# Three paddings in the on-chip memory of a hybrid pooling and attention layer

## The chip, the cores and the metric

The kernel runs on one core of one Trainium2 chip. A core has TensorE (matmuls: a stationary operand, the weights, is loaded first, and a moving operand then streams past it), VectorE, ScalarE, GpSimd and a sync engine that issues most of the transfers. Operands of the engines lie in the on-chip memory, which has 128 partitions; a place in it is a number of bytes from the start of each partition. Matmul results go to eight banks of PSUM.

The metric is the device time of one execution in microseconds (us), lower is better. The kernel before takes 1139.48 us, the median of 3 runs (1139.41 to 1140.89).

## What is computed

One decoder layer in float32, on a sequence of 1,024 rows of 1,024 channels:

```python
h = rms_norm(x, ln_pre_mix[l])
proj = h @ w_in[l]
...
q, k = rope(q, pos), rope(k, pos)
pool_out = multi_scale_pool(u_pool, w_pool[l], pool_scale[l])
attn_out = dilated_attention(q, k, v).reshape(B, S, ATTN_WIDTH)
mix = jnp.concatenate([pool_out, attn_out], axis=-1) @ w_out[l]
x = x + rms_norm(mix, ln_post_mix[l])
h = rms_norm(x, ln_pre_ffn[l])
f = (jax.nn.silu(h @ w_gate[l]) * (h @ w_up[l])) @ w_down[l]
x = x + rms_norm(f, ln_post_ffn[l])
```

The pooling mixer takes 256 channels, the attention 12 heads of 64 channels, each under three windows and strides. The feed-forward part is 2,816 wide (22 tiles of 128).

## The kernel before

Channels lie on the partitions and positions along the free dimension. Each float32 operand is split into a high part, rounded to the type float32r, and a low part, the rest; a product is three float32r matmuls (high by high, high by low, low by high: `PASSES`, L331). A big matmul has 128 x 128 weights and a moving operand of 128 x 512, so 2,048 bytes in each partition.

The stages follow each other: the input projection with the statistics of the first normalisation, the twelve attention units (a pair of heads and half of the positions each) with projections of later pairs as filling work between them, the output projection, and the feed-forward part. The two big products of the feed-forward part are done in Strassen's manner with seven block products instead of eight: `seven` (L1471) has, for each of 11 pairs of tiles, seven products of 2 x 4 x 3 matmuls. Three of these have a block of the normalised input itself as the moving operand (tiles `b00`, `b10`, `b11`, made by `block`, L1336; the profile calls them `b`), four a sum of blocks (tiles `tT1` to `tT4`; the profile calls them `tT`). For the first six pairs (`EARLY`) two of the products are made ahead by `firsts` (L1367). `down` (L1799) has seven products of 11 x 4 x 3 matmuls with operands from `operands` (L1643), the last of them in halves of 256 columns. `out_proj` (L1154) has 8 x 8 x 3 matmuls for each half of the positions; for one tile of them, d = 3 of the second half, the weights lie in the block `b4` of the `ffnl` pool (L1160). `rows_first` (L933) has the rows of `x` as weights and the weight matrix as the moving operand; two of its eight k-tiles lie in `w3` (L928). `turn` (L848) turns the score tiles `pp` with `idt` or `pmt` as the moving operand.

Every matmul goes through the helper `mm` (L275), which keeps TensorE's instructions in the order in which the program writes them. Splits into high and low parts are spread over ScalarE, VectorE and GpSimd by hand, and the order around them comes from the planner's due times in `PRM`.

The on-chip memory is a stack from each end. Pools on the left are placed upward in the order in which they are opened, pools with `side="right"` downward from the top, and a pool is as big as what its tiles need. Each tile is rounded up to 32 bytes. In the compiled program the left side begins with 2,048 bytes of transfer scratch and four constants of the framework; behind them come `const` (half, eps, ones, idt, g2s, g3s, g4s: from 2,176), `wpool` (two `wraw` of 4,096 bytes, from 2,880), `small` (from 11,072) and then, from 13,216, first `con1` (g1s, qdA, qdB, ls0, ls1, pmt, rb, psc) and `att`, and in the feed-forward part `ffnl` (r3, the blocks b0 to b5, three `rw`, two `q`). In `con1`, `pmt` lies at 14,336, `rb` at 14,848 and `psc` at 18,944; `att` begins at 18,976. `idt` lies at 2,272. The `ffnl` blocks begin at 17,312 and are 8,192 bytes each.

On the right the top is at 229,344. From there down come `xg` (eight tiles of 8,192 bytes: first `x0` to `x7`, later `z`, `tT`, `op` and others in the same places), `hlp` (two `whl`), and then `qkp` (k, qh, ql, masks and others) or, in the feed-forward part, `mid` (four `fw`, `sq`, `p`, `rb` strips).

The lines that the change touches are the opening of the pools, the tile of ones for the sums of squares, and the load of the pooling scale:

```python
xgp = ctx.enter_context(tc.tile_pool(name="xg", bufs=1, side="right"))
...
ones = const.tile([P, 1], F32, name="ones")
...
psc = cload(pscale, [P, 2], "psc", con1)
```

Of the kernel before, what the change touches and what calls it, by code (L numbers as in the profile page):

```python
# [8 lines left out]
F32 = mybir.dt.float32  # L9
# [6 lines left out]
P = 128  # L16
# [254 lines left out]
def hybrid_block(ctx: ExitStack, tc: tile.TileContext, xT, w_in, w_v, w_vp, w_pool, w_out, w_gate, w_up, w_down,  # L271
                 g1, g2, g3, g4, pscale, cost, sint, maskA, maskB, quadA, quadB, lsel, ident, perm, band, out):
    nc = tc.nc
# [6 lines left out]

    const = ctx.enter_context(tc.tile_pool(name="const", bufs=1))
    wpool = ctx.enter_context(tc.tile_pool(name="wpool", bufs=1))
    xgp = ctx.enter_context(tc.tile_pool(name="xg", bufs=1, side="right"))
    hlp = ctx.enter_context(tc.tile_pool(name="hlp", bufs=1, side="right"))
    small = ctx.enter_context(tc.tile_pool(name="small", bufs=3))
# [15 lines left out]
    def cload(src, shape, name, pool=None, eng=nc.sync):  # L301
        t = (pool or const).tile(shape, F32, name=name)
        eng.dma_start(t, src)
        return t
# [47 lines left out]
    right, left = ExitStack(), ExitStack()  # L352
    con1 = left.enter_context(tc.tile_pool(name="con1", bufs=1))
# [8 lines left out]
    for h in range(2):  # L362
        for a in range(2):
            nc.gpsimd.memset(qlow[h][64 - 64 * a:128 - 64 * a, a].bitcast(F32), 0.0)
    ones = const.tile([P, 1], F32, name="ones")
    nc.vector.memset(ones, 1.0)
    warm = qkp.tile([P, 512], F32R, name="warm", tag="rsw", bufs=1)
    nc.vector.memset(warm.bitcast(F32), 0.0)
# [645 lines left out]
        did(("pool", h))  # L1014

    g2s, g3s, g4s = (cload(g, [P, NK], "g%ds" % (n + 2)) for n, g in enumerate((g2, g3, g4)))
    psc = cload(pscale, [P, 2], "psc", con1)

    def emit(*lists):

# [904 lines left out]
```

## Time and profile before

| what | value |
|---|---|
| median of 3 runs | 1139.48 us |
| the profiled execution's own time | 1139.3 us |
| its span, first to last instruction | 1137.5 us |
| mean granted TensorE clock | 0.997 |
| matmuls in the trace | 5922 |
| data moved by transfers | 201.59 MB, 177 GB/s over the span |

In the views, PE is TensorE's matmuls, PEld its weight loads, DVE VectorE, ACT ScalarE, POOL GpSimd. Matmuls overlap each other: the duration of one (about 390 ns for 512 columns) is longer than the distance from its start to the start of the next, and it is this distance, the pace, that fills the time. The pace is read from a run of equal matmuls: the start of the next group less the start of this one, divided by the number; or the length of a piece in the chain in order of time, divided by its number.

A row of matmuls names `out<-moving,stationary`. All tiles of one name share a row, and so do all tiles whose names differ only in their number.

### The profile page before, as it was taken

To read this page: it belongs to the slowest core of one execution; us is meant where nothing else is said; L and a number is where in the kernel's file an instruction comes from. 1 tells how busy PE (TensorE), PEld (TensorE's weight loads), DVE (VectorE), ACT (ScalarE), POOL (GpSimd) and SP (SyncE) were. 2 spreads that over 40 slices of the span, in tenths; PEclk is the share of its full clock that TensorE was granted. 3 is DMA by queue.
4 is the path that set the end of the run, shared out by engine and by line. 5 is a ranking of instruction groups with operands and counts; after the bars stand their busy time and mean duration, and the time that the engine had idled before them with its cause. 6 is when DMAs were issued, how large, how long until landed. Compare 5 with 4: busy or idle time off the path is not lost.

```text
span 1137.5 us, 16902 instructions
## 1 busy us (share of the span) xinstructions
PE 1120.4 (98%) x5922; PEld 958.1 (84%) x5922; DVE 807.6 (71%) x1516; ACT 559.1 (49%) x1068; POOL 550.6 (48%) x481
## 2 busy tenths in 40 slices
PE   9999999999999999999999999999999999999997
PEld 7888999999898888888888878888888888888896
DVE  7967888888998675989777777665676473343684
ACT  7466667666678573965422222322323434344441
POOL 0122646253465222010267667775577897666521
PEclk9999999999999999999999999999999999999999
DMA  8215242414147555773566666433544796566442
GB/s 280 93 70 186 83 141 75 149 57 167 56 131 246 181 200 193 291 254 123 188 231 231 232 231 231 167 141 142 190 167 167 272 351 222 192 203 192 141 149 74
DMA packets 91156, 201.59 MB, mean 177 GB/s; under 512 B 9280, under 2 KB 25152, under 8 KB 89664
## 3 DMA queue, kind: packets, MB, share of 16 engines
q1 hardware_dynamic: 90096, 199.74, 50.2%
q8 instruction: 46, 0.75, 0.3%
q10 hardware_dynamic: 976, 0.79, 0.2%
q14 instruction: 38, 0.31, 0.1%
HBM read 143.61 MB, written 56.89 MB: 176 GB/s over the span
## 4 chain that ended last, share of the span: by engine, by line
PE 87%; DVE 6%; POOL 3%; DMA 2%; issue 1%; ACT 1%; SPq 0%; ACTq 0%; DVEq 0%; POOLq 0%
PE ps_pj L276 28%; PE ps_s L276 25%; PE ps_o L276 22%; PE ps_t L276 10%; PE ps_t L279 3%; DMA rw<-in_w_up_dram 1%; POOL fw L1365 1%; POOL pp L814 1%; DVE pp L748 1%; DVE ptr L860 1%; DVE rsw L510 0%; POOL whl L1464 0%; DMA wraw<-in_w_in_dram 0%; ACT pp L751 0%; DVE ql L542 0%
## 5 line engine op out<-in xcount | busy, mean ns | idle before, releaser
L276 PE MATMUL ps_o<-tT,fw 128*128 128x512 f32 x648 | 150.9, 390 | 0.9 <-DVE sq L1548 0.9
L276 PEld LDWEIGHTS ps_o<-tT,fw 128*128 128x128 f32 x648 | 121.5, 188 | 26.9 <-issue 1.3
L276 PE MATMUL ps_pj<-x,whl 128*128 128x512 f32 x480 | 138.1, 407 | 0.3 <-DVE whl L322 0.3
L814 POOL TENSOR_SCALAR pp<-pp,wv 128x256 f32<-128x256 f32 (+1 forms) x135 | 67.8, 523 | 111.5 <-DVE wv L794 111.5
L1365 POOL TENSOR_TENSOR fw<-rw,fw 128x512 fp32r<-128x512 f32 x72 | 100.3, 1416 | 30.2 <-ACT fw L1363 30.1
L751 ACT ACTIVATE pp<-pp,sx 128x128 f32<-128x128 f32 (+1 forms) x192 | 89.3, 468 | 31.5 <-DVE sx L748 30.9
L276 PEld LDWEIGHTS ps_pj<-x,whl 128*128 128x128 f32 x480 | 85.0, 189 | 11.2 <-DVE whl L322 0.7
L348 POOL TENSOR_TENSOR nrr<-nrr,half 128x4 f32<-128x4 f32 (+1 forms) x7 | 7.9, 1124 | 145.5 <-ACT eps L347 103.8
L1660 POOL TENSOR_TENSOR op<-rw,op 128x512 fp32r<-128x512 f32 x38 | 62.3, 1638 | 32.5 <-ACT op L1659 32.5
L322 POOL TENSOR_TENSOR whl<-wraw,whl 128x512 fp32r<-128x512 f32 x42 | 54.7, 1327 | 45.3 <-ACT whl L318 45.3
L276 PE MATMUL ps_s<-b,fw 128*128 128x512 f32 x312 | 74.6, 394 | 0.0
L276 PEld LDWEIGHTS ps_s<-b,fw 128*128 128x128 f32 x312 | 58.5, 187 | 14.2
L1365 POOL TENSOR_TENSOR whl<-rw,whl 128x512 fp32r<-128x512 f32 x30 | 47.1, 1589 | 44.2 <-ACT whl L1363 30.1
L276 PE MATMUL ps_pj<-whl,x 128*128 128x256 f32 (+1 forms) x432 | 68.4, 299 | 0.0
L1363 ACT ACTIVATE fw<-rw 128x1024 fp32r<-128x1024 f32 x45 | 47.5, 1061 | 41.8 <-PE ps_o L276 17.8
L1659 ACT ACTIVATE op<-rw 128x1024 fp32r<-128x1024 f32 x38 | 40.0, 1058 | 56.4 <-PE ps_t L276 28.2
L860 DVE TENSOR_TENSOR ptr<-ps_t,ptr 128x512 fp32r<-128x512 f32 (+1 forms) x84 | 55.3, 665 | 12.1 <-ACT ptr L859 11.3
L859 ACT ACTIVATE ptr<-ps_t 128x512 fp32r<-128x512 f32 (+1 forms) x84 | 47.4, 578 | 27.9 <-PE ps_t L279 24.0
L276 PEld LDWEIGHTS ps_pj<-whl,x 128*128 128x128 f32 x432 | 58.2, 191 | 1.7
L1661 DVE TENSOR_TENSOR op<-rw,op 128x512 fp32r<-128x512 f32 x33 | 28.8, 872 | 40.1 <-ACT op L1659 29.9
L276 PE MATMUL ps_o<-ptr,v 128*128 128x128 f32 (+1 forms) x472 | 56.4, 257 | 0.2 <-DVE ptr L860 0.2
L276 PE MATMUL ps_s<-k,qh 128*128 128x128 f32 (+1 forms) x192 | 54.4, 295 | 1.9 <-DVE sx L748 1.5
(328 smaller groups left out, 2858.7 us busy)
## 6 DMA issues: line engine op xcount, KB each, us to landing
rw<-bd SPq DMA_DIRECT2D x77, 256.0 KB, 4.0
rw<-in_w_gate_dram SPq DMA_DIRECT2D x28, 512.0 KB, 4.3
rw<-in_w_up_dram SPq DMA_DIRECT2D x28, 512.0 KB, 5.9
v<-vd SPq DMA_DIRECT2D x22, 512.0 KB, 4.6
rw<-wsd SPq DMA_DIRECT2D x44, 256.0 KB, 3.8
bd<-p SPq DMA_DIRECT2D x39, 256.0 KB, 2.1
rw<-in_w_down_dram SPq DMA_DIRECT2D x33, 256.0 KB, 3.8
wraw<-in_w_out_dram SPq DMA_DIRECT2D x15, 512.0 KB, 4.8
```

Of the source, the lines that this page charges most:

```text
L276: return tc.keep_in_program_order(nc.tensor.matmul(*a, **k))
L279: return tc.keep_in_program_order(nc.tensor.transpose(dst, src, by))
L322: pin(eng.tensor_tensor(dst[:, 1, at:at + w], src[:, at:at + w], dst[:, 0, at:at + w].bitcast(F32), ALU.subtract))
L751: nc.scalar.activation(pt[:, j, lo:], pt[:, j, lo:], AF.Exp, bias=sx[:, 0, side, j, hd, 0:1], scale=-1.0, accum_out=sx[:, 0, side, j, hd, ...
L814: nc.gpsimd.tensor_scalar(pv, pv, un.wv[:, side, j, hd:hd + 1], 1.0, op0=ALU.mult, op1=ALU.mult)
L859: nc.scalar.activation(ptr[:, 0, :w], t[:, :w], AF.Copy)
L860: nc.vector.tensor_tensor(ptr[:, 1, :w], t[:, :w], ptr[:, 0, :w].bitcast(F32), ALU.subtract)
L1363: nc.scalar.activation(dst[:, :, 0], src, AF.Copy)
L1365: low[0] = eng.tensor_tensor(dst[:, i, 1], src[:, i], dst[:, i, 0].bitcast(F32), ALU.subtract)
L1659: nc.scalar.activation(w[:, :, 0], raw, AF.Copy)
L1660: nc.gpsimd.tensor_tensor(w[:, 0, 1], raw[:, 0], w[:, 0, 0].bitcast(F32), ALU.subtract)
L1661: (nc.gpsimd if p == "P1" else nc.vector).tensor_tensor(w[:, 1, 1], raw[:, 1], w[:, 1, 0].bitcast(F32), ALU.subtract)
```

## The change

Three tiles of padding are added. A pool `edge` with one tile of 504 floats (2,016 bytes), that nothing reads or writes, is opened on the right ahead of `xg`. The tile of ones becomes 281 floats wide, and its first column is used. The tile of the pooling scale becomes 98 floats wide, and its first two columns are used; its load is written out instead of through `cload` (L301), on the same queue and at the same place.

```diff
     const = ctx.enter_context(tc.tile_pool(name="const", bufs=1))
     wpool = ctx.enter_context(tc.tile_pool(name="wpool", bufs=1))
+    edge = ctx.enter_context(tc.tile_pool(name="edge", bufs=1, side="right"))
+    edge.tile([P, 504], F32, name="edge")
     xgp = ctx.enter_context(tc.tile_pool(name="xg", bufs=1, side="right"))
...
-    ones = const.tile([P, 1], F32, name="ones")
+    ones = const.tile([P, 281], F32, name="ones")[:, :1]
     nc.vector.memset(ones, 1.0)
...
     g2s, g3s, g4s = (cload(g, [P, NK], "g%ds" % (n + 2)) for n, g in enumerate((g2, g3, g4)))
-    psc = cload(pscale, [P, 2], "psc", con1)
+    psc = con1.tile([P, 98], F32, name="psc")[:, :2]
+    nc.sync.dma_start(psc, pscale)
```

## The prediction

> **What bounds the kernel now.** I read the page first, then the busy time by stretches, then the chain of waits in order of time, then TensorE's timeline and the matmuls grouped by form.
>
> ```profile
> span 1137.5 us, 16902 instructions
> PE 1120.4 (98%) x5922; PEld 958.1 (84%) x5922; DVE 807.6 (71%) x1516; ACT 559.1 (49%) x1068; POOL 550.6 (48%) x481
> PE 87%; DVE 6%; POOL 3%; DMA 2%; issue 1%; ACT 1%; SPq 0%; ACTq 0%; DVEq 0%; POOLq 0%
> ```
>
> TensorE is busy for 1120.4 of 1137.5 us and makes 87% of the chain that ended last. Whatever changes the pace of one matmul to the next changes the end; whatever changes another engine's pace must first use up that engine's idle time.
>
> ```profile
> 200.00:340.00 140.00, 138.12 (x910) 126.27 (x909) 121.51 (x346) 94.98 (x250) 61.59 (x81) 1.00 0.34 113
> 480.00:620.00 140.00, 140.00 (x627) 114.37 (x627) 114.37 (x160) 62.54 (x96) 45.02 (x34) 1.00 0.58 203
> 700.00:800.00 100.00, 100.00 (x437) 81.61 (x436) 67.39 (x74) 29.24 (x35) 68.31 (x50) 1.00 0.45 172
> 800.00:900.00 100.00, 100.00 (x437) 81.60 (x437) 60.50 (x63) 28.12 (x35) 71.69 (x52) 1.00 0.53 192
> ```
>
> The columns are PE, weight loads, VectorE, ScalarE, GpSimd, then the granted clock, here 1.00. Even between 200 and 340 us TensorE idles for only 1.88 of 140 us. From 480 us on, it has no gap in these stretches, and each matmul there costs its full pace. That pace is not one number. In the timeline (start, length, group) and in the chain in order of time (start, length, number) stand runs of 24 or 48 matmuls of one shape:
>
> ```profile
> 454.76 5.66 PE L276 MATMUL ps_s<-fw,b 128*128 128x512 f32 x24
> 465.69 5.60 PE L276 MATMUL ps_s<-fw,whl 128*128 128x512 f32 x24
> 586.24 5.60 PE L276 MATMUL ps_s<-tT,whl 128*128 128x512 f32 x24
> 591.68 11.04 PE L276 MATMUL ps_o<-tT,fw 128*128 128x512 f32 x48
> 602.56 5.76 PE L276 MATMUL ps_s<-b,fw 128*128 128x512 f32 x24
> 608.16 5.62 PE L276 MATMUL ps_o<-tT,fw 128*128 128x512 f32 x24
> ```
>
> ```profile
> 454.92 5.49 PE ps_s L276 x24
> 465.85 5.44 PE ps_s L276 x24
> 540.94 11.20 PE ps_s L276 x48
> 586.40 5.44 PE ps_s L276 x24
> 591.84 10.88 PE ps_o L276 x48
> 602.72 5.60 PE ps_s L276 x24
> ```
>
> The names after the arrow are the moving tile, then the stationary one. With `tT` or `fw` moving, 24 matmuls take 5.44 us, 226.7 ns each. With `b` moving they take 5.60 us (48 take 11.20), 233.3 ns each. With `fw` moving and `b` stationary they take 5.49 us, 228.8 ns. The 48 `tT` matmuls at 591.84 and the 24 `b` matmuls that follow differ in nothing that the profile shows but the moving tile: both have `fw` as weights. The PSUM tag does not decide, since `ps_s` appears at both paces.
>
> What differs is where the tiles lie. The compiled program of the kernel before has every big right-hand tile (`x`, `tT`, `op`, `fw`, `whl`, `k`, `qh`) 2,016 bytes past a multiple of 2,048, the `ffnl` tiles (`b`, `rw`, `r3`) 928 past one, the `att` tiles (`pp`, `ptr`, `v`, `w3`) 544 past one. Weights start 512 bytes apart within their tile, so the distance from weights to moving tile, modulo 512, is 0 for right on right (226.7 ns), 448 for `b` moving over right (233.3 ns), and 64 for right over `b` (228.8 ns). A third pair has distance 64, `w3` moving over `x`:
>
> ```profile
> 53.43 2.91 PE L276 MATMUL ps_pj<-w,x 128*128 128x512 f32 x12
> 56.18 1.08 PE L276 MATMUL ps_t<-w,x 128*128 128x512 f32 x4
> ```
>
> Its 12 matmuls take 56.18 - 53.43 = 2.75 us, 229.2 ns each, the pace of the other pair at distance 64 within the rounding of the starts. `w3` lies on the left like `b`, among the same addresses, so the side itself does not make the pace. I read the pace as set by the distance between the two operands.
>
> **The change, part by part.** The three paddings add no instruction, and the scale vector's load keeps its queue, its place in line and its bytes. They move tiles. On the right, 2,016 bytes at the top move every pool down onto a multiple. On the left, `ones` grows from 32 bytes (with rounding) to 1,152, so that everything behind it moves by 1,120, and `ffnl` starts at 13,216 + 1,120 = 14,336, which is 7 times 2,048; `psc` adds 384 more ahead of `att`, which goes from 544 to 0 past a multiple (1,120 + 384 + 544 = 2,048). Two big tiles stay off: `wraw` at 4,000 and `rb` at 15,968.
>
> The `b` matmuls, from the grouping by form:
>
> ```profile
> L276 PE MATMUL ps_s<-b,fw x312: 393/394/398, 507.2 to 911.7; 128*128 128x512 f32 x156
> L276 PE MATMUL ps_pj<-b,fw x216: 393/394/398, 518.4 to 889.7; 128*128 128x512 f32 x108
> L276 PE MATMUL ps_pj<-b,whl x120: 390/394/478, 483.0 to 878.7; 128*128 128x512 f32 x120
> L276 PE MATMUL ps_t<-b,op x48: 393/396/398, 496.0 to 506.9; 128*128 128x512 f32 x48
> L276 PE MATMUL ps_t<-b,fw x48: 393/396/398, 529.6 to 540.5; 128*128 128x512 f32 x48
> L276 PE MATMUL ps_s<-b,whl x48: 394/394/394, 751.9 to 873.1; 128*128 128x512 f32 x48
> L276 PE MATMUL ps_s<-fw,b x24: 388/392/394, 454.8 to 460.0; 128*128 128x512 f32 x24
> ```
>
> That is 312 + 216 + 120 + 48 + 48 + 48 = 792 with `b` moving, and 24 with `b` as weights. After the change their distance is 0. Then the 792 fall from 233.3 to 226.7 ns: 792 x (5.60 - 5.44)/24 = 5.28 us. The 24 give 0.05 us, the 48 of `w3` (rows_first: 2 k-tiles x 3 passes x 8 row tiles) 48 x 2.5 ns = 0.12 us; together 5.4 us.
>
> What the trace does not show is a big operand that starts at the multiple itself, so the price of the right-hand move has two ends. The paces seen lie at most one step of 6.7 ns apart, so I bound it by one step down and one step up, for the 2,952 matmuls of 512 columns with a right-hand moving tile: 1,056 on `tT` (11 blocks x 4 products x 24), 792 in the down projection (6 products x 11 x 12), 384 in the output projection, 576 for queries and keys, 144 in rows_first. 2,952 x 6.67 ns is 19.7 us either way. I take zero, because right on right keeps distance 0, and distance sorts all the paces above.
>
> The Trainium skill's "TensorE: Matmul & The Clock Gate", section "Wait — 56ns, not 53.3ns?", gives 215.7 ns for such matmuls one behind the other; the trace's best steady pace, 226.7, lies 11 ns above it. If alignment were all of that gap, the estimate by that page would be 2,952 x 11.0 + 792 x 17.6 = 46 us less, about 1093. Its "SBUF — State Buffer", section "Who interferes with whom", gives TensorE two independent read ports and says that it never waits on anyone; by that, no distance between weights and moving tile could matter, and the sum would be zero. The 228.8 and 233.3 ns above disagree.
>
> The transposes mix: their weights (`pp`) move by 1,504 bytes, their moving tiles `idt` and `pmt` by 1,120.
>
> ```profile
> L279 PE MATMUL ps_t<-pmt,pp 128*128 128x128 f32 x180 | 27.2, 275 | 0.0
> L279 PE MATMUL ps_t<-idt,pp 128*128 128x128 f32 x144 | 21.9, 279 | 2.1 <-POOL pp L814 2.0
> ```
>
> `pmt` now lies at 14,336, exactly on a multiple, `idt` at 2,272, 224 past one, and they show 275 and 279 ns. Bound: one step of 6.7 ns each way for 324, 2.2 us; I take 0, since the two distances of today differ and their durations hardly do. `ptr` over `v` (both `att`) and `k` over `qh` (both right) keep their distance: 0.
>
> The other engines: ScalarE takes the same time for three placements of its input.
>
> ```profile
> L1363 ACT ACTIVATE fw<-rw 128x1024 fp32r<-128x1024 f32 x45 | 47.5, 1061 | 41.8 <-PE ps_o L276 17.8 <-PE ps_s L276 9.7 <-DMA wsd<-fw 8.9
> L318 ACT ACTIVATE whl<-wraw 128x1024 fp32r<-128x1024 f32 x37 | 39.1, 1057 | 16.0 <-PE ps_pj L276 11.1 <-DMA wraw<-in_w_vp_dram 1.6 <-PE ps_t L276 1.3
> L415 ACT ACTIVATE jk<-xraw 128x1024 f32<-128x1024 f32 x7 | 7.4, 1052 | 1.0 <-DVE sq L417 1.0
> ```
>
> `rw`, `wraw` and `xraw` lie 928, 832 and 544 past a multiple, and 1061, 1057 and 1052 ns follow. I cost them at 0, hidden behind TensorE besides. DMA landings get 0 as well. That cover is thinnest where the chain leaves TensorE for a load:
>
> ```profile
> 641.45 6.19 DMA rw<-in_w_up_dram
> 665.81 7.07 DMA rw<-in_w_up_dram
> ```
>
> A TensorE that arrives earlier there waits for `rw` and the operands made from it. The `b` stretches between 620 and 680 us are two, so at most 48 x 6.67 ns = 0.3 us is given back.
>
> Sum against the profiled execution: 1139.3 us, of which 1.8 lie around the span. 1137.5 - 5.4 + 1.8 = 1133.9; the median shown is 0.2 above that execution, so 1134.1, and I say 1134.0. With the transposes' 2.2 us, the 0.3 and rounding its own range is 1131.5 to 1136.5.
>
> **The rivals.**
>
> *A further step for everything.* A start at the multiple is worth one more step of 6.67 ns for all 3,744 big matmuls: 1134.0 - 3,744 x 6.67 ns (25.0) = 1109. For it: no operand of these now starts there, and the tiles were all off by 32 bytes or more. Against it: the pace of the right-hand matmuls is the same for weights at all four 512-byte places, and `pmt` on its multiple runs hardly faster than `idt`.
>
> *Slower: common starts collide.* The moving stream and the weight load that overlaps it begin rows on the same boundary; if that costs a step, the right-hand matmuls go to 233.3 as `b` has it today, and `b` stays: 1139.4 + 19.7 = 1159. It outweighs the gain from 5.4 / 0.00667 = 810 matmuls on, 27% of the 2,952. For it: the change gives the whole memory one phase. Against it: modulo 512 the right-hand side already has one phase and is the fastest case.
>
> *No change.* The pace of `b` comes from something that moves with it (its rows' distance to other traffic, the stage), or only absolute placement on the right matters and cancels. Time 1139.5. Against it: `b` keeps 5.60 us in stretches with GpSimd at 45.02 of 140 us and at 71.69 of 100 us alike. That the change does not do what it says belongs here: `wraw` and `rb` stay off, but no big matmul reads them.
>
> **How the numbers follow.** Distance alone (1134) 0.58, the further step (1109) 0.20, no change 0.09, slower (1159) 0.13. A measurement here tells about 0.2% (2.3 us) from no change: below 1137.2 is faster, above 1141.8 slower. Faster holds the first two, 0.78; same 0.09; slower 0.13. The range must reach from the further step to no change to leave out 0.13 only: 1108 to 1140. Beside it stands the likeliest case's own, 1131.5 to 1136.5.
>
> **What would show it.** In the chain, runs of 24 with `b` moving at 5.44 instead of 5.60 us and the run at 454.92 at 5.44 instead of 5.49: right; `tT` runs still at 5.44. `tT` runs at 5.28: the further step. `tT` at 5.60: the slower rival. `b` still at 5.60 would make the distance reading wrong, and with it the prediction. ScalarE's 1061 ns and the transposes' 275 and 279 should stay.

## The result, and the profile after

| | before | after |
|---|---|---|
| median, same chip | 1140.26 us, 6 runs (1139.41 to 1141.07) | 1134.49 us, 6 runs (1133.22 to 1135.39) |
| profiled execution's own time | 1139.3 us | 1133.22 us |
| its span | 1137.5 us | 1131.4 us |
| mean granted clock | 0.997 | 0.998 |

The ratio of after to before is 0.9946, with a 95% interval of 0.9934 to 0.9958: the kernel is 5.8 us faster, and the time lies 0.5 us above the predicted 1134.0.

The changed kernel's page, its span, its engines and the shares of the chain that ended last:

```profile
span 1131.4 us, 16902 instructions
PE 1115.9 (99%) x5922; PEld 958.3 (85%) x5922; DVE 806.1 (71%) x1516; ACT 559.9 (49%) x1068; POOL 549.0 (49%) x481
PE 90%; DVE 5%; DMA 2%; POOL 1%; ACT 1%; issue 1%; ACTq 0%; SPq 0%; POOLq 0%
```

The instructions are the same in number on every engine, and PE holds more of the chain than before. The span is 6.1 us shorter and PE's busy time 4.5 us, so some 1.6 us of PE's idle time has gone as well.

The chain in order of time (start, length, engine, tag, line, number), with the pieces that answer to those of before:

```profile
455.32 5.44 PE ps_s L276 x24
466.20 5.44 PE ps_s L276 x24
539.80 10.88 PE ps_s L276 x48
584.74 5.44 PE ps_s L276 x24
590.18 10.88 PE ps_o L276 x48
601.06 5.44 PE ps_s L276 x24
```

Before, the run with `b` as weights took 5.49 us (first line), the 48 with `b` moving 11.20 (third) and the 24 with `b` moving 5.60 (last). Now every run of 24 takes 5.44 us and every run of 48 takes 10.88, 226.7 ns for one matmul. The three runs that were at 5.44 or 10.88 before have stayed there. TensorE's timeline names the operands of three of these runs, and of the matmuls with `w3`:

```profile
53.10 2.88 PE L276 MATMUL ps_pj<-w,x 128*128 128x512 f32 x12
55.82 1.07 PE L276 MATMUL ps_t<-w,x 128*128 128x512 f32 x4
...
455.15 5.60 PE L276 MATMUL ps_s<-fw,b 128*128 128x512 f32 x24
...
590.02 11.04 PE L276 MATMUL ps_o<-tT,fw 128*128 128x512 f32 x48
600.90 5.60 PE L276 MATMUL ps_s<-b,fw 128*128 128x512 f32 x24
```

A group's length here includes the long tail of its last matmul, so the pace is read from start to start: 600.90 - 590.02 = 10.88 us for 48 with `tT`. The 12 with `w3` take 55.82 - 53.10 = 2.72 us, 226.7 ns each, against 2.75 before.

Busy time by stretches (PE, weight loads, VectorE, ScalarE, GpSimd, granted clock, DMA share, GB/s), after:

```profile
480.00:620.00 140.00, 140.00 (x637) 116.09 (x636) 116.13 (x161) 64.06 (x96) 46.17 (x35) 1.00 0.59 210
620.00:700.00 80.00, 80.00 (x355) 66.26 (x354) 59.68 (x70) 20.22 (x23) 59.31 (x43) 1.00 0.65 232
700.00:800.00 100.00, 100.00 (x442) 82.65 (x441) 68.83 (x75) 31.11 (x37) 71.44 (x51) 1.00 0.44 166
800.00:900.00 100.00, 100.00 (x443) 82.79 (x442) 58.43 (x64) 30.63 (x36) 72.40 (x54) 1.00 0.55 198
```

A gain in pace does not show as idle time. PE is still busy for the whole of each stretch, but 637, 442 and 443 matmuls start in the stretches where 627, 437 and 437 did before, at the same clock of 1.00. The second stretch before was:

```profile
620.00:700.00 80.00, 79.07 (x347) 64.69 (x346) 58.08 (x68) 21.01 (x24) 59.58 (x43) 1.00 0.63 226
```

Here TensorE idled for 0.93 us before and not at all after. It is the stretch in which the chain of before left TensorE for two loads into `rw`. After the change the chain has no such piece.

Two of the rows of `b` matmuls after, grouped by form (three durations: low, median, high; then first and last start):

```profile
L276 PE MATMUL ps_s<-b,fw x312: 389/389/390, 507.0 to 905.4; 128*128 128x512 f32 x156
L276 PE MATMUL ps_pj<-b,whl x120: 387/389/486, 483.3 to 872.8; 128*128 128x512 f32 x120
```

The first `b` matmul of the feed-forward rounds starts at 483.3 us, against 483.0 before, so nothing has been gained up to there. The last one starts at 905.4 us instead of 911.7, so the gain lies between the two.

### The profile page after: what moved, and what is told of

The parts are those of the page before. It is cut to its first block, busy times and chain, and to the rows that moved or that the text cites. A ratio compares the mean times of both kernels' runs of the same rounds, so it can differ in the third digit from the quotient of the medians.

```text
span 1131.4 us, 16902 instructions
## 1 busy us (share of the span) xinstructions
PE 1115.9 (99%) x5922; PEld 958.3 (85%) x5922; DVE 806.1 (71%) x1516; ACT 559.9 (49%) x1068; POOL 549.0 (49%) x481
## 4 chain that ended last, share of the span: by engine, by line
PE 90%; DVE 5%; DMA 2%; POOL 1%; ACT 1%; issue 1%; ACTq 0%; SPq 0%; POOLq 0%
PE ps_pj L276 27%; PE ps_s L276 26%; PE ps_o L276 24%; PE ps_t L276 10%; PE ps_t L279 2%; DMA mixd<-mix 1%; POOL pp L816 1%; DVE pp L750 1%; DVE ptr L862 1%; DMA m<-mixd 1%; DVE rsw L512 0%; ACT pp L753 0%; DVE ql L544 0%; DMA wraw<-in_w_in_dram 0%; DVE rco L513 0%
## 5 line engine op out<-in xcount | busy, mean ns | idle before, releaser
L1366 ACT ACTIVATE fw<-rw 128x1024 fp32r<-128x1024 f32 x45 | 47.5, 1061 | 41.4 <-PE ps_o L276 16.3
```

The costliest lines, as they stand in the source:

```text
L1366: nc.scalar.activation(dst[:, :, 0], src, AF.Copy)
```

## The experiments

The theory is the prediction's: the pace of a matmul of 512 columns is set by the distance between the starts of its two operands. The distance is the moving tile's start less the weights' start, modulo a period that was taken as 512 bytes. The main rival is that the multiple of 2,048 itself does it. Open beside these were the period, the shape of the price between the known distances, and whether a wrong distance between other tiles costs as much.

**A common start off the multiple** (`common928`). The kernel before, with one padding on the right only, so that the right-hand tiles lie 928 bytes past a multiple of 2,048, as `ffnl` does. No big tile that matmuls of the feed-forward part read lies on a multiple.

```diff
+    edge = ctx.enter_context(tc.tile_pool(name="edge", bufs=1, side="right"))
+    edge.tile([P, 272], F32, name="edge")
```

> Only one padding of 1,088 bytes on the right, so that the right-hand tiles lie 928 bytes past a multiple of 2,048, where the ffnl blocks already are; nothing at all lies on a multiple. Distance theory: weights and b are 0 apart modulo 512, so runs of 24 matmuls with b moving take 5.44 us instead of 5.60, tT stays at 5.44, and the time is that of the changed kernel, about 1134.5 us (ratio 0.995 to the kernel before). Own-place theory (a moving tile at 928 is slow by itself): b stays at 5.60 and tT, op, fw and x go to 5.60 too, up to 19.7 us more, about 1159. Third reading (a multiple of 2,048 is what matters): no better than before, 1140.

Measured: 1135.64 us (6 runs, 1134.38 to 1136.97), ratio 0.9954 (0.994 to 0.9969). Its chain in order of time, for the runs with `tT`, `tT` and `b` moving:

```profile
740.58 5.44 PE ps_s L276 x24
746.02 5.44 PE ps_o L276 x24
751.46 5.44 PE ps_s L276 x24
```

The `b` run is as fast as with starts on the multiple, at a place that is no multiple of anything above 32. So the multiple is not needed for the faster pace. The matmuls with `w3` over `x`, at distance 128 here (544 - 928 = -384), show about 232 ns, slower than the 229 of before: a gain for one pair was a loss for another.

**On the multiple, at the old distance** (`far448`). The changed kernel with `edge` 64 bytes smaller: `b` keeps its place on the multiple of 2,048, the right-hand tiles lie 64 past one, and the distance from the right-hand weights to `b` is 448 again.

```diff
-    edge.tile([P, 504], F32, name="edge")
+    edge.tile([P, 488], F32, name="edge")
```

> Both left paddings as in the changed kernel, so that b lies on a multiple of 2,048, but the right-hand padding 64 bytes shorter, so that weights lie 64 past one: the distance from weights to b is 448 modulo 512, as in the kernel before. Distance theory: b back at 5.60 us for 24, tT at 5.44, time that of the kernel before, about 1140 (ratio 1.000); w3 over x, now at 448 too, at 233 ns. Own-place theory: b on its multiple is fast, 5.44 us, and the time is about 1134.5.

Measured: 1139.57 us (10 runs), ratio 0.9997 (0.9988 to 1.0006). Its chain, for `tT`, `tT`, `b` and `b` moving:

```profile
740.63 5.44 PE ps_s L276 x24
746.07 5.44 PE ps_o L276 x24
751.51 5.60 PE ps_s L276 x24
757.10 5.60 PE ps_pj L276 x24
```

`b` on its multiple takes 5.60 us, and the whole gain is gone. Together with the run before, this parts distance from place on both sides: common starts off the multiple give the gain, starts on the multiple at distance 448 do not.

**Which distances cost** (`scan_a`, `scan_b`). In the changed kernel each block of the input begins a chosen number of bytes into a larger tile, so that `b00`, `b10` and `b11` stand at three distances from the same weights in one run.

```diff
-        return ffnl.tile(shape, dt, name=name, tag="b%d" % n)
+        t = ffnl.tile([P, 2176], dt, name=name, tag="b%d" % n)
+        at = OFF[n // 2] // 4
...
+        return t[:, at:at + 2048].rearrange("p (a b c) -> p a b c", b=shape[2], c=shape[3])
```

`OFF` holds the bytes for `b00`, `b10` and `b11`: 128, 192, 256 in the first, 320, 384, 480 in the second.

> The changed kernel with the blocks of b moved within ffnl: b00 128 bytes, b10 192 and b11 256 past the weights, modulo 512. Distance theory: each of the three has a pace of its own, between 226.7 and 240 ns, and if the pace follows the distance smoothly, 128 lies near the 228.8 of 64 and 256 is the farthest; a pace below 226.7 at some distance would mean that 0 is not the best. Own-place theory with multiples of 2,048 alone as the good place: all three at 233.3. The tT runs stay at 5.44 us.

> As before with 320 bytes for b00, 384 for b10 and 480 for b11. Distance theory: paces of their own, 384 and 480 near the 233.3 of 448 if the pace follows the distance smoothly; own-place theory: all three at 233.3.

Measured: 1138.06 and 1138.11 us, one run each. In a late round the products come in the order `b11`, `b00`, a `tT`, `b10`. The chain of the first, with distances 256, 128, 0 and 192:

```profile
751.50 5.44 PE ps_s L277 x24
756.93 5.59 PE ps_pj L277 x24
762.53 5.45 PE ps_o L277 x24
767.98 5.60 PE ps_pj L277 x24
```

The chain of the second, with distances 480, 320, 0 and 384:

```profile
749.88 5.60 PE ps_s L277 x24
755.48 5.49 PE ps_pj L277 x24
760.98 5.46 PE ps_o L277 x24
766.44 5.59 PE ps_pj L277 x24
```

Distance 256 is as good as 0, 320 takes what 64 took before (5.49), and 384 takes what 128 takes (5.59). The period is 256 bytes, not 512. Both guesses in the first expectation for a smooth price missed: 128 does not lie near the 228.8 ns of 64, and 256 is not the farthest distance but a best one.

**A wrong distance for the other matmuls** (`apart192`). The changed kernel with 192 bytes between `xg` and `hlp`, so that `tT`, `x` and `b` stand at 192 from the weights in `fw` and `whl`, while the tiles of the down projection (`op`, `fw` and `whl`), each of which holds weights and moving operand together, stay at 0 over themselves. No start of a matmul operand in `xg` or `ffnl` moves.

```diff
+    gap = ctx.enter_context(tc.tile_pool(name="gap", bufs=1, side="right"))
+    gap.tile([P, 48], F32, name="gap")
     hlp = ctx.enter_context(tc.tile_pool(name="hlp", bufs=1, side="right"))
```

> The changed kernel with 192 bytes of gap between xg and everything right of it in the stack, so that weights in whl and fw lie 64 bytes past a multiple of 256 and tT, x and b on one: distance 192 modulo 256. Distance theory with the paces seen so far (period 256: 192 gives 233.3 ns): runs of 24 with tT go from 5.44 to 5.60 us, and so does b over fw and whl; b over op, and op and fw over themselves, stay at 5.44. 1,056 of tT and 744 of b cost 1,800 x 6.67 ns = 12.0 us after 480 us; 576 of the queries and keys and 168 of the output projection cost 5.0 more where TensorE sets the pace there, and 192 at distance 64 cost 0.4. Between 1147 and 1152 us, the higher if the input and output projection pass their loss on. Own-place theory, or a theory that only b was odd: 1134.5, since tT, x and b lie on multiples as in the changed kernel.

Measured: 1147.73 us (4 runs, 1146.24 to 1148.63), ratio 1.0065 (1.0045 to 1.0084). Its chain, for three runs with `tT` and one with `b`:

```profile
740.58 5.60 PE ps_o L276 x24
746.18 5.60 PE ps_s L276 x24
751.78 5.60 PE ps_o L276 x24
757.38 5.60 PE ps_s L276 x24
```

The `tT` runs, which stayed at 5.44 to 5.47 us in the kernels so far, are at 5.60. The stretch from the first `b` matmul to the 5,001st matmul of the trace, which lies in the down projection, is 12.1 us longer than in the changed kernel (475.26 against 463.13 us, start to start), as worked out for it.

Two parts of the expectation missed. Ahead of that stretch only 2.3 us were lost (the first `b` matmul starts at 485.6 us, after: 483.3), about 3 us less than expected, so the total lies at the low end. From start to start, the 576 matmuls of the queries and keys take 143.50 us instead of 141.79 and the 168 of the output projection 41.01 instead of 40.52: 2.2 us, where 5.0 was expected. So more than half of the price did not arise there. These matmuls stand in shorter runs among others, and for `x` over `whl` the median distance from one start to the next is 231 ns even in the changed kernel, against 234 here; why it is 231 at distance 0 was not tried.

The other miss is the down projection, which was expected to keep its pace. It changes its tile every 12 matmuls. In TensorE's timeline each tile has four groups of three; these are the first groups of three tiles in turn:

```profile
947.06 0.85 PE L276 MATMUL ps_pj<-fw 128*128 128x512 f32 x3
949.82 0.86 PE L276 MATMUL ps_pj<-op 128*128 128x512 f32 x3
952.55 0.85 PE L276 MATMUL ps_pj<-fw 128*128 128x512 f32 x3
```

The 12 on `fw` take 2.76 us and the 12 on `op` 2.73, where 12 take 2.72 in the changed kernel. The four groups of that `fw` take 0.69, 0.69, 0.70 and 0.68 us. From the first start to the last, the 792 take 183.25 us instead of 181.61. Each of these matmuls has distance 0 to its own weights; what has changed is that one tile and the next now differ by 64 or 192 bytes modulo 256. So a switch between such tiles costs something too, and the distance to a matmul's own weights does not say everything.

**The smallest padding** (`small_pads`). The kernel before with `ones` at 96 bytes, `psc` at 160 and no `edge`: `ffnl` and `att` move by 64 and 192 bytes, to 992 and 736 past a multiple of 2,048, while the right stays at 2,016. The distances are 1,024 and 1,280, both 0 modulo 256 and neither side on a multiple. The padding is 64 + 128 = 192 bytes in place of 2,016 + 1,120 + 384 = 3,520.

```diff
-    ones = const.tile([P, 1], F32, name="ones")
+    ones = const.tile([P, 24], F32, name="ones")[:, :1]
...
-    psc = cload(pscale, [P, 2], "psc", con1)
+    psc = con1.tile([P, 40], F32, name="psc")[:, :2]
+    nc.sync.dma_start(psc, pscale)
```

> The kernel before with two small left paddings and none on the right: ones 96 bytes instead of 32 and the pooling scale 160 instead of 32, 192 bytes in all instead of 3,520. Everything then lies 224 past a multiple of 256, nothing on a multiple of 2,048, and all distances are 0 modulo 256 (not all modulo 512). Distance theory with period 256: the whole gain, about 1134.5 us, ratio 0.995. Theory that a period of 512 or multiples of 2,048 are needed: part of the gain or none, 1137 to 1140.

Measured: 1133.9 us (6 runs, 1132.96 to 1136.06), ratio 0.9948 (0.9933 to 0.9962). Its chain has `tT`, then `b` twice, all at the fast pace:

```profile
742.56 5.44 PE ps_o L276 x24
748.00 5.44 PE ps_s L276 x24
753.44 5.44 PE ps_pj L276 x24
```

The whole gain is there; 0.9948 and 0.9946 cannot be told apart. The multiples of 2,048 add nothing to it.

**Distances that are no multiple of 64** (`scan_c`, `scan_d`). The edit of the scans, with `OFF` 32, 96, 160 and then 16, 8, 240.

> b00 32 bytes, b10 96 and b11 160 past the weights. Distance theory with period 256: paces between those of the neighbours (0: 226.7, 64: 228.9, 128: 232.6, 192: 233.3 ns), so about 227 to 229, 229 to 232.6, and 233. If a distance that is no multiple of 64 were a price of its own, all three lie at 233.3.

> b00 16 bytes, b10 8 and b11 240 past the weights. Distance theory: 16 and 8 at 226.7 or below; 240 at 233.3 as 192 and 224, or already back towards 226.7 if the way from 224 to 256 is a slope. A pace below 226.7 would make another distance than 0 the best one and a faster kernel possible.

Measured: 1139.09 and 1139.59 us, one run each. The chain of the first, with distances 160, 32, 0 and 96:

```profile
751.25 5.62 PE ps_s L277 x24
756.87 5.60 PE ps_pj L277 x24
762.47 5.48 PE ps_o L277 x24
767.95 5.61 PE ps_pj L277 x24
```

The chain of the second, with distances 240, 16, 0 and 8:

```profile
752.15 5.60 PE ps_s L277 x24
757.75 5.56 PE ps_pj L277 x24
763.30 5.47 PE ps_o L277 x24
768.77 5.60 PE ps_pj L277 x24
```

The expectation of a price that rises smoothly with the distance was wrong: distances that are no multiple of 64 have a price of their own. Eight bytes cost as much as 192, and 32 costs more than 64. Of the distances that were run, only 64 (2.1 ns) and, less so, 16 (5.0 ns) cost less than 128 does.

The lengths of the runs of 24 above, sorted by distance modulo 256:

| distance | 0 | 64 | 128 | 192 | 8 | 16 | 32 | 96 | 160 | 224 | 240 |
|---|---|---|---|---|---|---|---|---|---|---|---|
| us for 24 | 5.44 | 5.49 | 5.59 | 5.60 | 5.60 | 5.56 | 5.60 | 5.61 | 5.62 | 5.60 | 5.60 |
| ns for one | 226.7 | 228.8 | 232.9 | 233.3 | 233.3 | 231.7 | 233.3 | 233.8 | 234.2 | 233.3 | 233.3 |

The ends of a run are given to 0.01 us, which is 0.4 ns for one matmul, so differences of that size in the table say nothing.

## Why the prediction was right

**The mechanism.** That `b` and its weights lay at a bad distance was right, and the runs show it from both sides: the gain without the multiple (`common928`, `small_pads`), and the multiple without the gain (`far448`). The reading needed one pair of rows from the kernel before, `tT` and `b` over the same weights in the same round, and a third pair at a distance that had already occurred, `w3` over `x`, to rule out the side of the memory. The period of 512 bytes was wrong, it is 256; this did no harm, since the change puts these operands at 0 modulo both.

**The 5.28 us for the 792 matmuls.** The pace fell from 233.3 to 226.7 ns, as worked out. Summed from start to start, the 792 take 179.88 us instead of 185.05, 5.17 less, and 179.88 in `common928` and `small_pads` as well. So the term was right to 0.1 us. From the first `b` matmul to the 5,001st matmul the time fell by more, from 469.77 to 463.13 us, by 6.6. The rest is in the 1,056 `tT` matmuls, 239.72 us instead of 241.17, and has two parts.

Some 0.35 us of it is a price that the prediction put at nothing: in the kernel before, a `tT` run that follows a `b` run is slowed too (5.46 us at 608.32 us in its chain), and after the change it takes 5.44.

About 1.1 us is a single wait of the execution before, near 679 us, that is missing after the change: it is the 0.93 us of idle time shown above, and 1.31 us pass there from one start to the next. The prediction had feared the opposite there, up to 0.3 us given back at the loads. The pace of `b` does not decide this wait: `common928` and `small_pads` have the same pace as the changed kernel, and yet TensorE idles for 0.44 and 0.63 us between 620 and 700 us, and the chain of each still leaves it for one load into `rw` (at 666.35 and 662.51 us). Their stretches are 464.11 and 464.31 us, 5.7 and 5.5 us less than before. Whether the placement decides it or it varies from one execution to the next is open.

Behind that matmul the difference moves by about 1 us and was not traced: the last matmul starts 5.3 us earlier than before, and the span ends 6.1 us earlier. The median lies within 0.5 us of the forecast, while the six runs after the change spread over 2.2 us, so that closeness is in part luck.

**The right-hand move at zero.** It was priced between -19.7 and +19.7 us, and zero was right: away from a slow `b` run, `tT` runs are at 5.44 us with starts 2,016, 0, 928 and 64 past a multiple of 2,048, as long as their weights stand at distance 0.

**The transposes and the other engines at zero.** The transposes after, grouped by form:

```profile
L279 PE MATMUL ps_t<-pmt,pp 128*128 128x128 f32 x180 | 27.2, 275 | 0.0
L279 PE MATMUL ps_t<-idt,pp 128*128 128x128 f32 x144 | 21.8, 276 | 2.0 <-POOL pp L816 2.0
```

275 and 276 ns against 275 and 279 make 27.2 and 21.8 us against 27.2 and 21.9: zero. In the same view, ScalarE takes 1061 ns for a `rw` that now begins on the multiple, as before, and 1056 for `wraw`, which still lies off, against 1057.

**The rivals.** The further step needed `tT` runs at 5.28 us; none is below 5.44 in any of the ten kernels with starts on and off the multiple. The slower rival, common starts that collide, is the wrong way round: common starts are the best distance. It had named a real size, though. What it feared for the right-hand matmuls is what `apart192` does to the `tT` matmuls on `fw` and `whl`, by the distance instead of the start. No change fell with the `b` runs.

Two rules of the Trainium skill were weighed. In its "TensorE: Matmul & The Clock Gate", section "Wait — 56ns, not 53.3ns?", stands a pace of 215.7 ns; the best steady pace in these kernels is 226.7 ns at every start that was run, so alignment closes none of that gap, and what makes it was not tried. Its "SBUF — State Buffer", section "Who interferes with whom", gives weights and moving operand a read port each and says that TensorE never waits on anyone. Here the pace of the same instruction goes from 226.7 to 233.3 ns by the distance between the two alone, so for these matmuls that rule does not hold as it stands.

What stays open is the mechanism behind the distance. A weight load runs while the matmul before streams: after the change, in the rows of `ps_s<-b,fw`, the first load starts at 506.8 us and takes some 188 ns, and its matmul starts at 507.0. The weights of a tile follow each other at 512 bytes, a whole number of periods, so in a steady run a matmul has the same distance to its own weights and to the next ones, and no run here tells the two apart. Neither explains the down projection in `apart192`, where both are 0 for all but the last matmul on a tile, and the price of a switch still lasts over several matmuls.

## What to carry to other kernels

Where TensorE is the bound, compare the pace of equal matmuls that differ only in their tiles, from start to start; two paces at one granted clock point to the placement. Then work out the distance between the starts of weights and moving tile: here a multiple of 256 bytes was best, and any other that was run cost 1 to 3% of each 512-column float32r matmul in a long run. A padding of some tens of bytes in a small tile ahead is enough, but each pool that holds an operand has to be looked at as a pair with every other one, since what mends one pair can spoil the next, as it did for `w3` in `common928`.

## What the hardware showed beyond that

The price does not grow with the distance: 8 bytes cost 6.6 ns and 64 bytes 2.1, while 192, which is 64 to the other side, costs 6.6. The asymmetry and the jump are unexplained.

Matmuls of 256 columns did not pay. The rows of `whl` over `x`, grouped by form, in `apart192` at distance 64:

```profile
L276 PE MATMUL ps_pj<-whl,x 128*128 128x256 f32 x384 | 55.4, 287 | 0.0
```

and in the changed kernel at distance 0:

```profile
L276 PE MATMUL ps_pj<-whl,x 128*128 128x256 f32 x384 | 55.7, 288 | 0.0
```

Busy time is 55.4 us at the worse distance and 55.7 at the better one, where 2.1 ns for each of 384 would have added 0.8 us. They stand in short runs among other matmuls, so this does not show what a long run of 256 columns would do, and other distances were not run for them.

The `tT` run behind a `b` run at a bad distance takes 5.45 to 5.48 us in the scans, and 5.46 in the kernel before, instead of 5.44, though its own distance is 0; it is not seen where `b` is at distance 0. The cost reaches a little into the run that follows, as it does behind each change of tile in the down projection of `apart192`.
